# Head sums of both recurrence norms by exact block matrices in two passes, roots between 32x32 block transposes on VectorE

## The chip, the core and the metric

The kernel runs on one core of a Trainium2 chip. TensorE multiplies matrices (128 rows of contraction, results in PSUM banks of 512 fp32 columns), VectorE and ScalarE work on rows of 128 partitions, POOL and SyncE mostly issue transfers. Each engine takes its instructions in a fixed order, and waits between engines are semaphores. The metric is device time in microseconds (us); less is better. The time before is 1618.17 us, the median of three runs (1615.87 to 1621.76).

## The reference, cut to what matters

One layer of a hybrid decoder runs over 1024 prompt tokens and 8 groups of 8 sample tokens, 1088 columns in all. The change touches two norms of the recurrence branch, both over heads of 64 features:

```python
kk = heads(k * lp["k_k"])
kk = kk * lax.rsqrt(jnp.sum(kk * kk, axis=-1, keepdims=True) + 1e-12)
...
y, wkv_new = wkv7_scan(wkv_prev.astype(f32), rh, heads(decay), kh, vh, kk, ah)
mean = jnp.mean(y, axis=-1, keepdims=True)
var = jnp.mean(jnp.square(y - mean), axis=-1, keepdims=True)
y = ((y - mean) * lax.rsqrt(var + GN_EPS)).reshape(B, T, MIX_WIDTH)
y = y * lp["ln_w"].astype(f32) + lp["ln_b"].astype(f32)
bonus = jnp.sum(rh * kh * lp["r_k"].astype(f32), axis=-1, keepdims=True) * vh
y = (y + bonus.reshape(B, T, MIX_WIDTH)).astype(pr.dtype) * g
```

There are 8 heads, hence four blocks of 128 features (two heads each), f = 0 to 3. Around this stand one large input projection (1024 features to 4352), a pooling branch, a gated merge, an output projection and a squared-ReLU MLP.

## The kernel before, in words

Features lie on partitions and tokens along the free axis, so a row tile is 128 x 1088. The large products run in three single-pass products each: weights and activations are split into a high part (hi, rounded to the fp32r type) and a rest (lo), and hi x hi, hi x lo, lo x hi are summed in PSUM.

The first phase (`phase1`, up to about 755 us) has a *background* and *foreground* work on TensorE. The background is the input projection: 34 output blocks in two halves, 12 products for each three column chunks (364, 362, 362; `mm<-hx,whi` and `mm<-hx,wlo` in the trace), 2448 products, then 288 more for the merge's pooling part (`op_job`), 2736 in all. Its weights come as 128x512 loads on SyncE (L216) and are split by ScalarE (hi, L227) and VectorE or POOL (lo, L228); each split serves 36 products. The foreground is a set of generators: `chains`, `pools` (the pooling branch, one group of channels at a time: products, ScalarE copy L683, VectorE L684), `heads` (the recurrence) and `or_rows`. A planner, `Pace`, writes the program: it adds up a modelled time for every TensorE instruction and resumes a generator when its due time has come (`yield 2500` asks for 2.5 us of modelled time to pass); else it puts the next background product. So the order on TensorE is what the yields make it, and it is kept as written; the other engines' orders come from a scheduler. `pace.fill` puts one background triple between two foreground instructions.

`heads` goes through the four blocks. `front(f)` makes the normed key kk; `burst`, `scores`, `unit`, `bonus` prepare the products within chunks of 64 tokens; `inverse`, `level` and `affine` invert the chunks' triangular blocks; `chain` carries the state over the chunks (a state copy S on ScalarE, L1086, between TensorE products); `sample` does the sample tokens; `post(f)` is the group norm with scale, shift, bonus and gate. `post(f-1)` and `front(f+1)` run as a second generator beside `inverse`, `level` and `affine` of block f (`both`). `level` has a VectorE transpose (L961) whose result the next TensorE products (`hv,ao`) need.

The norms before. `rinv` is called nine times: in four fronts, three posts, and twice for the last post, which is done in two halves. Each call has for each 128 tokens a TensorE product with the *data block as weights* and two columns (`hsel`, one for each head) moving, in pairs between background triples. This gives the sums with tokens on partitions: 128 x 18 for the whole row. ScalarE takes the root (L396, with a table load), VectorE the reciprocal (L397), ScalarE expands each to 64 columns (L401) and loads the table of Tanh again by a dummy (L403); `spread` then transposes the expanded blocks back on TensorE (helper `tr`, L211), and VectorE multiplies from PSUM (L720 in the front, L1216 in the post). The mean of the post is an fp32 product with a 0/1 block matrix `bones` (helper `mm`, L204, `w<-wt,kct`), subtracted by VectorE (L1205) and squared by ScalarE (L1206); L1218 and L1219 add the shift and bonus and apply the gate; L1238 and L1239 split the result into hi and lo. The fp32r type is taken in one pass; these fp32 products are not.

At the end of the first phase the merge's operands come back by SyncE loads of 544 KB (`hx<-d_op`, L1416; `hx<-d_or`, L1428), and stored gate rows are reloaded on ScalarE's queue (`px<-d_th`, L1436).

The second phase (merge, output projection, MLP) keeps its TensorE instructions and their order.

## Time and profile before

| what | value |
|---|---|
| runs, median | 1618.17 us (1615.87 to 1621.76) |
| profiled execution | 1622.76 us, span 1621.0, mean granted TensorE clock 0.989 |
| TensorE busy | 1576.7 us, 97% |
| VectorE, ScalarE, POOL busy | 63%, 45%, 22% |
| stage 75 to 645 us (background and heads) | PE 561.18 of 570 |
| stage 645 to 755 us (last block, merge loads) | PE 104.16 of 110, clock 0.94 |

A row of a group reads: line, engine, operation, output<-inputs, shapes, count | busy us, mean ns of one | idle time ahead of it and what ended it. L204 and L211 are helpers that record every product and every transpose, so their groups are told apart by the tile names. An fp32 product has two records.

### The profile page before, as it was taken

The page shows a single profiled execution, that of the slowest core. Times are in us where ns is not written, and L with a number is a line of the kernel's source. Part 1 is how long each engine was busy: PE and PEld are TensorE (multiplying, and loading weights), DVE is VectorE, ACT ScalarE, POOL GpSimd, SP SyncE. Part 2 cuts the span into 40 slices and gives each one's busy share as a digit, 9 for nine tenths or more (in the row PEclk, how much of TensorE's full clock was granted, in tenths as well). Part 3 has the DMA queues.
Part 4 walks back from the last instruction along what each step waited for, and adds up shares of the span by engine and source line. Part 5 has one row for each costly group of instructions (what it writes and reads, how often), then busy time and mean ns, then how long its engine had stood idle before and what let it go on. Part 6 is the DMA issues. An engine that isn't in the chain of part 4 may idle for free.

```text
span 1621.0 us, 35482 instructions
## 1 busy us (share of the span) xinstructions
PE 1576.7 (97%) x14331; PEld 1472.5 (91%) x14331; DVE 1020.1 (63%) x1747; ACT 734.6 (45%) x1491; POOL 358.1 (22%) x464
## 2 busy tenths in 40 slices
PE   6999999999999999999999999999999999999997
PEld 3999878997898889879989999999999999999997
DVE  5685574756565636334635587776555677787866
ACT  5543343354334434432325475554445765553323
POOL 3301210020001000101513322333233343521221
PEclk9999999999999999899999999999999999999998
DMA  9334314333413242836874465667666965674313
GB/s 336 108 120 157 134 58 132 108 101 112 152 67 114 90 144 91 296 121 210 328 273 166 143 215 199 205 231 257 223 204 227 321 201 183 199 265 154 101 40 111
DMA packets 123380, 279.43 MB, mean 172 GB/s; under 512 B 16816, under 2 KB 31152, under 8 KB 123216
## 3 DMA queue, kind: packets, MB, share of 16 engines
q1 hardware_dynamic: 107856, 228.52, 41.2%
q0 software_dynamic: 9312, 32.41, 6.0%
q10 hardware_dynamic: 6048, 16.23, 2.9%
q8 instruction: 113, 1.85, 0.5%
q14 instruction: 51, 0.42, 0.1%
HBM read 198.15 MB, written 78.95 MB: 171 GB/s over the span
## 4 chain that ended last, share of the span: by engine, by line
PE 58%; DVE 3%; ACT 3%; issue 3%; DMA 2%; POOL 1%; POOLq 0%; ACTq 0%; SPq 0%; DVEq 0%
PE pr L204 30%; PE mm L204 20%; PE w L204 4%; PE wc L204 3%; DVE hx L1847 1%; DMA wraw<-in_w_out 1%; DMA d_hid<-hx 0%; DMA d_th<-px 0%; ACT whi L227 0%; POOL wlo L228 0%; PE w L211 0%; ACT hx L1770 0%; ACT mr L1770 0%; DVE wlo L228 0%; DMA d_orl<-wt 0%
## 5 line engine op out<-in xcount | busy, mean ns | idle before, releaser
L204 PE MATMUL mm<-hx,whi 128*128 128x362 f32 (+1 forms) x1920 | 509.6, 347 | 0.7 <-ACT px L573 0.7
L204 PEld LDWEIGHTS mm<-hx,whi 128*128 128x128 f32 x1920 | 333.5, 191 | 31.3 <-issue 13.0
L204 PE MATMUL pr<-mr,whi 128*128 128x272 f32 x1792 | 336.2, 287 | 0.2 <-DVE hx L1847 0.2
L204 PE MATMUL mm<-hx,wlo 128*128 128x362 f32 (+1 forms) x960 | 316.4, 330 | 0.0
L204 PEld LDWEIGHTS pr<-mr,whi 128*128 128x128 f32 x1792 | 280.6, 188 | 2.1 <-issue 2.1
L204 PE MATMUL pr<-mr,wlo 128*128 128x272 f32 x896 | 257.8, 288 | 0.0
L227 ACT ACTIVATE whi<-wraw 128x512 fp32r<-128x512 f32 x186 | 116.9, 629 | 204.6 <-PE mm L204 68.1
L228 DVE TENSOR_TENSOR wlo<-wraw,whi 128x512 fp32r<-128x512 f32 x145 | 108.4, 748 | 123.7 <-ACT whi L227 122.8
L204 PEld LDWEIGHTS mm<-hx,wlo 128*128 128x128 f32 x960 | 183.4, 191 | 0.0
L204 PE MATMUL pr<-hx,whi 128*128 128x272 f32 x896 | 168.8, 287 | 2.3 <-ACT hx L1650 0.9
L204 PEld LDWEIGHTS pr<-mr,wlo 128*128 128x128 f32 x896 | 168.6, 188 | 0.0
L204 PE MATMUL mm<-mr,whi 128*128 128x272 f32 (+4 forms) x736 | 152.3, 301 | 0.0
L204 PEld LDWEIGHTS pr<-hx,whi 128*128 128x128 f32 x896 | 140.2, 188 | 3.8 <-ACT hx L1650 1.1
L227 ACT ACTIVATE whi<-wr 128x512 fp32r<-128x512 f32 x138 | 86.3, 627 | 115.3 <-PE pr L204 76.7
L204 PE MATMUL pr<-hx,wlo 128*128 128x272 f32 x448 | 128.9, 288 | 0.0
L204 PEld LDWEIGHTS mm<-mr,whi 128*128 128x128 f32 x736 | 119.2, 188 | 3.0 <-issue 2.5
L204 PE MATMUL mm<-mr,wlo 128*128 128x272 f32 (+4 forms) x368 | 110.1, 299 | 0.0
L228 POOL TENSOR_TENSOR wlo<-wraw,whi 128x512 fp32r<-128x512 f32 x41 | 55.6, 1356 | 216.4 <-ACT whi L227 216.3
L228 DVE TENSOR_TENSOR wlo<-wr,whi 128x512 fp32r<-128x512 f32 x103 | 77.2, 752 | 19.2 <-ACT whi L227 19.2
L204 PE MATMUL pr<-t,whi 128*128 128x272 f32 x448 | 84.7, 287 | 0.7 <-DVE hx L1670 0.7
L204 PEld LDWEIGHTS pr<-hx,wlo 128*128 128x128 f32 x448 | 84.3, 188 | 0.0
L204 PEld LDWEIGHTS pr<-t,whi 128*128 128x128 f32 x448 | 70.1, 188 | 1.8 <-issue 1.8
(467 smaller groups left out, 2714.0 us busy)
## 6 DMA issues: line engine op xcount, KB each, us to landing
wr<-in_w_ff SPq DMA_DIRECT2D x137, 256.0 KB, 3.5
hid<-d_ch POOLq DMA_DIRECT2D x72, 272.0 KB, 3.8
wraw<-in_w_ff SPq DMA_DIRECT2D x71, 256.0 KB, 3.1
wraw<-in_w_in SPq DMA_DIRECT2D x68, 256.0 KB, 2.9
d_ch<-hx SPq DMA_DIRECT2D x52, 272.0 KB, 3.7
hid<-in_w_ada_mlp SPq DMA_DIRECT2D x24, 512.0 KB, 6.2
d_th<-px SPq DMA_DIRECT2D x22, 544.0 KB, 3.0
wt<-d_x SPq DMA_DIRECT2D x20, 544.0 KB, 3.8
```

Of the source, the lines that this page charges most:

```text
L204: return self.nc.tensor.matmul(out, lhsT, rhs, **kw)
L227: nc.scalar.activation(hi, raw, AF.Copy)
L228: (nc.gpsimd if pool else nc.vector).tensor_tensor(lo, raw, hi.bitcast(F32), op=ALU.subtract)
L1847: nc.vector.tensor_tensor(acc, acc, v, op=ALU.add)
```

## The change

Two helpers replace the old chain. `head_sums` makes the head sums as two fp32r products with a 0/1 block matrix that this type holds exactly: one with the data's hi part moving, one with its lo part, summed in PSUM. Every feature row of a head then holds the head's sum, with tokens along the free axis, so nothing has to be expanded. `apart` makes hi (ScalarE copy) and lo (VectorE subtraction). For the mean a second matrix `cen` (identity less 1/64 in each head's block) gives the centred value in the same two products; ScalarE squares it twice (once as fp32, once rounded) and copies it back, and VectorE makes the lo part of the square.

The roots: VectorE transposes the sums from PSUM in 32x32 blocks, so that one column of each block holds 32 different tokens; ScalarE takes the root of these columns (128 x 34 for the whole row), VectorE the reciprocal, and one VectorE transpose of the broadcast gives full rows again (128 x 1088, tile `e`). Then one multiplication of the whole row takes the place of the pieces.

The counts on TensorE: 72 products with two columns, 72 transposes and 12 fp32 mean products go; 72 fp32r products come, 24 of 512 and 48 of 288 columns. ScalarE's program has 15 instructions more, VectorE's 26. `bones` and `cen` are loaded on the POOL queue and rounded by ScalarE; the bonus sum keeps its fp32 product. hi and lo use the `wt` buffers. The bonus row's load moves behind `rinv` in the first three posts. The yields of the planner around all this change, and the order of pool and gate blocks in the background with them (two lines below stand for the yields). In the second phase nothing changes.

```diff
+KEEP = KC["bones"][0]
...
+    same = (r // 64) == (np.arange(P)[None] // 64)
+    put("bones", same)
+    put("cen", np.eye(P) - same / 64.0)
...
-    def rinv(self, x, blocks, scale, eps, R):
-
-        nc, k = self.nc, len(blocks)
-        ps = self.ps("w")
-        for i, b in enumerate(blocks):
-            if i and i % 2 == 0:
-                self.pace.fill()
-            self.mm(ps[:, 2 * i:2 * i + 2], x[:, b:b + 128], self.kc("hsel"), start=True, stop=True)
-        r = self.cp.tile([P, 10, 2], F32, tag="rh", bufs=3, name=self.nm("rh"))
-        last, r = r[:, 9, 0:1], r[:, :k, :]
-        f = r.rearrange("p k h -> p (k h)")
-        nc.scalar.activation(f, ps[:, :2 * k], AF.Sqrt, bias=self.eps[:, eps:eps + 1], scale=scale)
-        nc.vector.reciprocal(f, f)
-        i = 0
-        for x in R:
-            m = x.shape[1] // 128
-            nc.scalar.activation(x.rearrange("p (k h j) -> p k h j", h=2, j=64), r[:, i:i + m, :].unsqueeze(3).to_broadcast([P, m, 2, 64]), AF.Copy)
-            i += m
-        nc.scalar.activation(last, R[-1][:, 0:1], AF.Tanh)
-        return [x[:, o:o + 128] for x in R for o in range(0, x.shape[1], 128)]
-
-    def spread(self, R):
-
-        ps = self.ps("w")
-        for i, x in enumerate(R):
-            self.tr(ps[:, i * 128:(i + 1) * 128], x, self.kc("ident"))
-        return ps
+    def head_sums(self, w, hi, lo, s):
+
+        ps, n = self.ps("w"), s.stop - s.start
+        self.mm(ps[:, :n], w, hi[:, s], start=True, stop=False)
+        self.mm(ps[:, :n], w, lo[:, s], start=False, stop=True)
+        return ps[:, :n]
+
+    def rinv(self, x, hi, lo, cuts, scale, eps):
+
+        nc, a, b = self.nc, cuts[0].start // 32, cuts[-1].stop // 32
+        for s in cuts:
+            nc.vector.transpose(x[:, s], self.head_sums(self.bones, hi, lo, s))
+            yield 500
+        r = self.cp.tile([P, 2, 34], F32, tag="rh", bufs=2, name=self.nm("rh"))
+        q, r = r[:, 0, :b - a], r[:, 1, :b - a]
+        nc.scalar.activation(q, cut32(x)[:, a:b, 0], AF.Sqrt, bias=self.eps[:, eps:eps + 1], scale=scale)
+        nc.vector.reciprocal(r, q)
+        nc.scalar.activation(q[:, 0:1], q[:, 0:1], AF.Tanh)
+        nc.vector.transpose(cut32(x)[:, a:b, :], r.unsqueeze(2).to_broadcast([P, b - a, 32]))
+
+    def apart(self, x, hi, lo, s):
+
+        nc = self.nc
+        nc.scalar.activation(hi[:, s], x[:, s], AF.Copy)
+        nc.vector.tensor_tensor(lo[:, s], x[:, s], hi[:, s].bitcast(F32), op=ALU.subtract)
+
+    def wtr(self):
+        return self.row(self.p1, "wt", 5, F32R)
+
+    def spare(self):
+        return self.row(self.p1, "e", 1, w=1112)[:, :NT]
 
...
-            yield (8500, 9800, 9800, 10800)[g]
+            yield (9500, 11000, 11500, 10800)[g]
...
-        kk = self.wt()
+        sq, hi, lo = self.spare(), self.wtr(), self.wtr()
         for c0, n in FH:
-            nc.scalar.activation(kk[:, c0:c0 + n], k[:, c0:c0 + n], AF.Square, scale=self.par("k_k", f))
+            nc.scalar.activation(sq[:, c0:c0 + n], k[:, c0:c0 + n], AF.Square, scale=self.par("k_k", f))
+            self.apart(sq, hi, lo, slice(c0, c0 + n))
         yield X(12)
         wa = self.wt()
         nc.sync.dma_start(wa, self.d_x[12])
-        t1, tha = self.wt(), self.wt()
-        yield self.pace.warm(FW if f else 11000)
-
-        R = self.rinv(kk, self.blocks(0, NT), 1.0, 1, [kk[:, 0:512], kk[:, 512:1024], t1[:, 0:128]])
-        yield 2500
-        for i, (c0, n) in enumerate(((0, 512), (512, 512), (1024, 64))):
-            ps = self.spread(R[4 * i:4 * i + 4])
-            o = 64 if i == 2 else 0
-            nc.vector.scalar_tensor_tensor(kk[:, c0:c0 + n], k[:, c0:c0 + n], self.par("k_k", f), ps[:, o:o + n], op0=ALU.mult, op1=ALU.mult)
-            yield 800
+        yield FW if f else 14500
+
+        yield from self.rinv(sq, hi, lo, FS, 1.0, 1)
+        kk, t1, tha = self.wt(), self.wt(), self.wt()
+        nc.vector.scalar_tensor_tensor(kk, k, self.par("k_k", f), sq, op0=ALU.mult, op1=ALU.mult)
+        yield 1000
...
-            self.mm(ps[:, :n], self.kc("bones"), q[:, c0:c0 + n], start=True, stop=True)
+            self.mm(ps[:, :n], self.bones.bitcast(F32), q[:, c0:c0 + n], start=True, stop=True)
...
-        yield self.pace.warm(3000)
+        yield self.pace.warm(3500)
...
-        sq = self.wt()
-        bv = self.wt()
-        nc.sync.dma_start(bv, self.d_bv[f])
-        if not last:
+        hi, lo, sq = self.wtr(), self.wtr(), self.spare()
+
+        def bonus():
+            bv = self.wt()
+            nc.sync.dma_start(bv, self.d_bv[f])
+            return bv
+
+        if last:
+            bv = bonus()
+        else:
             if f < 2:
                 self.got = self.fetch(f + 2)
-            yield 5000
+            self.apart(y, hi, lo, slice(0, NT))
+            yield 5200
...
-            for a, m in FP:
-                if c0 <= a < c0 + n:
-                    s = slice(a, a + m)
-                    ps = self.ps("w")
-                    self.mm(ps[:, :m], self.kc("bones"), y[:, s], start=True, stop=True)
-                    nc.vector.scalar_tensor_tensor(y[:, s], ps[:, :m], -1.0 / 64, y[:, s], op0=ALU.mult, op1=ALU.add)
-                    nc.scalar.activation(sq[:, s], y[:, s], AF.Square)
-                    yield 1500
-            yield self.pace.warm(2500 if last else 3500)
-            end = c0 + n == NT
-            R = self.rinv(sq, self.blocks(c0, n), 1.0 / 64, 2, [sq[:, a:a + 512] for a in (0, 512) if c0 <= a < c0 + n] + [g2] * end)
-            yield 3000 if last else 4000
-            for i, a in enumerate(a for a in (0, 512) if c0 <= a < c0 + n):
-                for b, m, o, blk in ((a, 512, 0, R[4 * i:4 * i + 4]), (NPR, 64, 64, R[-1:]))[:1 + (a > 0)]:
-                    ps = self.spread(blk)
-                    t = y[:, b:b + m]
-                    nc.vector.scalar_tensor_tensor(t, t, self.par("ln_w", f), ps[:, o:o + m], op0=ALU.mult, op1=ALU.mult)
-                s = slice(a, NT if a else 512)
-                nc.vector.scalar_tensor_tensor(y[:, s], y[:, s], self.par("ln_b", f), bv[:, s], op0=ALU.add, op1=ALU.add)
-                nc.vector.tensor_tensor(y[:, s], y[:, s], sg[:, s], op=ALU.mult)
-                yield 1000
+            cuts = [x for x in FS if c0 <= x.start < c0 + n]
+            if last:
+                for x in cuts:
+                    self.apart(y, hi, lo, x)
+                yield 2000
+            for x in cuts:
+                ps = self.head_sums(self.cen, hi, lo, x)
+                nc.scalar.activation(sq[:, x], ps, AF.Square)
+                nc.scalar.activation(hi[:, x], ps, AF.Square)
+                nc.scalar.activation(y[:, x], ps, AF.Copy)
+                nc.vector.tensor_tensor(lo[:, x], sq[:, x], hi[:, x].bitcast(F32), op=ALU.subtract)
+                yield 800
+            yield 2500 if last else 3500
+            yield from self.rinv(sq, hi, lo, cuts, 1.0 / 64, 2)
+            s, b = slice(c0, c0 + n), bv if last else bonus()
+            nc.vector.scalar_tensor_tensor(y[:, s], y[:, s], self.par("ln_w", f), sq[:, s], op0=ALU.mult, op1=ALU.mult)
+            nc.vector.scalar_tensor_tensor(y[:, s], y[:, s], self.par("ln_b", f), b[:, s], op0=ALU.add, op1=ALU.add)
+            nc.vector.tensor_tensor(y[:, s], y[:, s], sg[:, s], op=ALU.mult)
...
          else:
+            yield 1500
             yield from norm(0, NT)
-            hi, lo = sq.bitcast(F32R), y.bitcast(F32R)
+            lo = y.bitcast(F32R)
             nc.scalar.activation(hi, y, AF.Copy)
             nc.vector.tensor_tensor(lo, y, hi.bitcast(F32), op=ALU.subtract)
             nc.sync.dma_start(self.d_or[0][f], hi.bitcast(F32))
...
-        for g in range(4):
-            jobs += [Q[g], G[2 * g], G[2 * g + 1]] if g < 3 else [G[6], Q[3], G[7]]
-        jobs += G[8:]
+        gates = iter(G)
+        jobs += [Q[int(x)] if x in "0123" else next(gates) for x in "0gg1gggg2ggg3"]
+        jobs += list(gates)
...
+        two = sm.tile([P, 2 * P], F32R, name="bones")
+        raw = self.hv()[:, :2 * P]
+        nc.gpsimd.dma_start(raw, io["kc"][:, KEEP:])
+        nc.scalar.activation(two, raw, AF.Copy)
+        self.bones, self.cen = two[:, 0:P], two[:, P:]
...
-FW = 5500
+FW = 8500
```

On TensorE, at the second block's norm. `wc_5970` collects the sums of squares, `mm` is background:

```order
L204 MATMUL mm_5795<-hx_352,wlo_5687 128x362
L204 MATMUL wc_5970<-kct,wt_5588 128x2 x2
L204 MATMUL mm_5793<-hx_354,whi_5759 128x364
L204 MATMUL mm_5793<-hx_355,whi_5759 128x364
L204 MATMUL mm_5793<-hx_354,wlo_5760 128x364
```

and some 30 instructions later a pool group's last products (`px`, `ds` with `plw`), the transposes of the roots and the products of a later block's inverse (`z,hv`):

```order
L204 MATMUL w_6058<-px_5615,plw_5222 128x298
L204 MATMUL w_6058<-ds_5786,plw_5222 128x64
L211 MATMUL wc_6063<-kct,wt_5588 128x128 x4
L204 MATMUL wc_6071<-z,hv_6042 32x32 x32
L211 MATMUL w_6108<-kct,wt_5588 128x128 x4
L211 MATMUL w_6114<-kct,sw_5582 128x128
L204 MATMUL mm_5794<-hx_358,whi_5759 128x362
```

Now the sums of the same norm (`wt_5527` is hi, `wt_5528` lo) between products of the inverse:

```order
L206 MATMUL wc_5730<-hv_5669,hv_5509 32x32 x64
L206 MATMUL wc_5797<-wt_5527,bones 128x512
L206 MATMUL wc_5797<-wt_5528,bones 128x512
L206 MATMUL mm_5617<-hx_358,whi_5607 128x362
L206 MATMUL mm_5617<-hx_359,whi_5607 128x362
L206 MATMUL mm_5617<-hx_358,wlo_5608 128x362
L206 MATMUL mm_5618<-hx_358,whi_5607 128x362
L206 MATMUL mm_5618<-hx_359,whi_5607 128x362
L206 MATMUL mm_5618<-hx_358,wlo_5608 128x362
L206 MATMUL w_5807<-wt_5527,bones 128x288
L206 MATMUL w_5807<-wt_5528,bones 128x288
```

The pool group's products no longer stand here, and nothing on TensorE comes back for the roots.

On VectorE, beside block 3's `level`. Before, with the mean subtractions (`wc_7536` to `w_7594`) and the transpose (L961):

```order
L1205 SCALAR_TENSOR_TENSOR wt_7432<-wc_7536,wt_7432 128x512
L1205 SCALAR_TENSOR_TENSOR wt_7432<-wc_7564,wt_7432 128x288
L228 TENSOR_TENSOR wlo_7574<-wraw_7571,whi_7573 128x512
L1205 SCALAR_TENSOR_TENSOR wt_7432<-w_7594,wt_7432 128x288
L954 TENSOR_TENSOR hv_7672<-w_7607,kct 128x512
L228 TENSOR_TENSOR wlo_7766<-wraw_7763,whi_7765 128x512
L961 STREAM_TRANSPOSE hv_7757<-wc_7692 128x512
L397 RECIPROCAL rh_7803<-rh_7803 128x18
L1216 SCALAR_TENSOR_TENSOR wt_7432<-wt_7432,part,wc_7938 128x512
```

Now, with the three transposes of the sums, the reciprocal, the transpose of the roots and L965, the former L961:

```order
L230 TENSOR_TENSOR wlo_7467<-wraw_7464,whi_7466 128x512
L958 TENSOR_TENSOR hv_7555<-wc_7490,kct 128x512
L398 STREAM_TRANSPOSE e_7293<-w_7557 128x512
L398 STREAM_TRANSPOSE e_7293<-w_7567 128x288
L398 STREAM_TRANSPOSE e_7293<-wc_7577 128x288
L403 RECIPROCAL rh_7652<-rh_7652 128x34
L405 STREAM_TRANSPOSE e_7293<-rh_7652 128x1088
L965 STREAM_TRANSPOSE hv_7646<-wc_7581 128x512
L1226 SCALAR_TENSOR_TENSOR wt_7284<-wt_7284,part,e_7293 128x1088
```

The transpose for the inverse stood ahead of the reciprocal and now stands behind the whole chain of the roots.

At the end of the first phase, on ScalarE, with the state copies S and the reload of a gate row. Before:

```order
L227 ACTIVATE whi_8096<-wraw_8094 128x512
L1086 ACTIVATE S_8155<-wc_8121 128x64
L1436 DMA px_8396<-d_th_101 128x1088
L1086 ACTIVATE S_8182<-wc_8121 128x64
L1086 ACTIVATE S_8197<-wc_8121 128x64
```

Now:

```order
L1090 ACTIVATE S_8167<-wc_7949 128x64
L1099 ACTIVATE wt_7272<-wc_7950 128x512
L410 ACTIVATE wt_8046<-wt_7272 128x512
L1450 DMA px_8268<-d_th_99 128x1088
L1090 ACTIVATE S_8237<-wc_8203 128x64
```

On SyncE, the merge's loads and the last gate row's write there (`d_th_105`), before:

```order
L1428 DMA hx_7884<-d_orh_74 128x1088
L1428 DMA hx_7886<-d_orl_78 128x1088
L1428 DMA hx_7888<-d_orh_75 128x1088
L1428 DMA hx_7890<-d_orl_79 128x1088
L608 DMA d_th_105<-px_7581 128x1088
L216 DMA wraw_8264<-in_w_br 128x512
L1186 DMA wt_8228<-d_bv_69 128x1088
```

Now:

```order
L1442 DMA hx_8144<-d_orh_74 128x1088
L1442 DMA hx_8146<-d_orl_78 128x1088
L1442 DMA hx_8148<-d_orh_75 128x1088
L1442 DMA hx_8150<-d_orl_79 128x1088
L1442 DMA hx_8152<-d_orh_76 128x1088
L1442 DMA hx_8154<-d_orl_80 128x1088
L614 DMA d_th_105<-px_7801 128x1088
L218 DMA wraw_8373<-in_w_br 128x512
```

All six loads of recurrence rows now stand ahead of that write; before, two came later.

More of the change, by code (lines that the diff above doesn't have):

```diff
@@ L541, in rest @@
                 round_(qi, 1)
-                yield from vectors(qi, 2600 if qi == 1 else 1800)
+                yield from vectors(qi, 2100 if qi == 1 else 1300)
                 rows(qi)
@@ L1060, in affine @@
         self.done.add(("s", f, 1))
-        yield 3600
+        yield 3300
     def chain(self, f, d):
@@ L1158, in sample @@
             ums.append(um)
-        yield 4500
+        yield 5000
         pn = self.ps("w")
@@ L1330, in run @@
             nc.gpsimd.dma_start(self.part, io["par"])
-            self.kct = self.cp.tile([P, NKC], F32, name="kct")
-            nc.gpsimd.dma_start(self.kct, io["kc"])
+            self.kct = self.cp.tile([P, KEEP], F32, name="kct")
+            nc.gpsimd.dma_start(self.kct, io["kc"][:, :KEEP])
             self.eps = self.cp.tile([P, 3], F32, name="eps")
```

12 lines of the change are left out of this document (6 added, 6 removed).

## Prediction

> **What bounds the kernel now.** I read the page first (busy shares, the forty slices, the chain that ended last), then a table by stage, then the chain and the timelines around each norm, then the costliest groups of VectorE and ScalarE by shape.
>
> ```profile
> span 1621.0 us, 35482 instructions
> PE 1576.7 (97%) x14331; PEld 1472.5 (91%) x14331; DVE 1020.1 (63%) x1747; ACT 734.6 (45%) x1491; POOL 358.1 (22%) x464
> PE   6999999999999999999999999999999999999997
> PE 58%; DVE 3%; ACT 3%; issue 3%; DMA 2%; POOL 1%; POOLq 0%; ACTq 0%; SPq 0%; DVEq 0%
> ```
>
> TensorE is busy 97% of the span and the chain that ended last runs mostly over it, so a microsecond less on TensorE is a microsecond less in the end, unless a wait takes its place. VectorE has a third of its time free, ScalarE half. By stage (the columns are length, busy time and instructions of PE, PEld, DVE, ACT and POOL, granted clock, DMA share, GB/s):
>
> ```profile
> 75.00:645.00 570.00, 561.18 (x6185) 496.94 (x6184) 351.45 (x651) 242.46 (x582) 47.72 (x99) 0.99 0.34 112
> 645.00:755.00 110.00, 104.16 (x1276) 92.94 (x1275) 40.09 (x74) 38.60 (x78) 9.78 (x9) 0.94 0.56 198
> 755.00:910.00 155.00, 154.41 (x1152) 147.87 (x1151) 82.45 (x134) 56.08 (x93) 53.65 (x52) 1.00 0.70 250
> ```
>
> The change acts in the first two rows, where background products and the head pipeline share TensorE. There 570.0 - 561.2 + 110.0 - 104.2 = 14.6 us are idle. The rest is work, so that is where most of a gain must come from. Everything after 755 us keeps its instructions; I cost it at nothing.
>
> **Removed from TensorE.** First the sums of squares, the block of data as weights and two columns moving, in pairs between three background products (start, duration, two records for each product); then one mean product of 288 columns; then transposes of the expanded roots in the last norm.
>
> ```profile
> 494.59 0.50 PE L204 MATMUL wc<-kct,wt 128*128 128x2 f32 x4
> ...
> 495.53 0.50 PE L204 MATMUL wc<-kct,wt 128*128 128x2 f32 x4
> 481.97 0.65 PE L204 MATMUL wc<-wt,kct 128*128 128x288 f32 x2
> ...
> 482.95 0.49 PE L204 MATMUL mm<-hx,whi 128*128 128x362 f32 x2
> 746.36 0.44 PE wc L211 x4
> 746.80 0.11 PE w L211
> 746.91 7.94 PE mm L204 x48
> 944.97 179.84 PE pr L204 x1443
> ```
>
> A background product of 362 columns takes 7.94 / 48 = 0.165 us, three 0.50. A pair and three background products take 495.53 - 494.59 = 0.94, so one sum product is (0.94 - 0.50) / 2 = 0.22; there are 72: 15.8 us. The mean product and three background products take 482.95 - 481.97 = 0.98, so 288 columns cost 0.48, and 512 by the same rate 0.48 x 512 / 288 = 0.85; 8 and 4 of them: 7.3 us. Five transposes take 746.91 - 746.36 = 0.55, or 0.11 each; 72: 7.9 us. Together 31.0 us.
>
> **Added to TensorE.** 72 single-pass products (hi and lo for each of three pieces, over nine root chains and the four centrings), 24 of 512 and 48 of 288 columns. No product of before in this form has these widths; the nearest are the background's own: 0.165 for 362 columns, and 179.84 / 1443 = 0.1246 for 272, both 0.00046 a column. So 288 columns cost 0.132 and 512 0.234: 6.3 + 5.6 = 11.9 us. From below 10% less (no fixed part); from above the price of the fp32 means, 48 x 0.48 + 24 x 0.85 = 43.4. I take the low end, since products of this type are the row it is nearest to. Net: -19.1 us.
>
> **The stall in the second block's norm.** Before, the root chain and a pool group met (chain pieces, PE timeline, and three windows with PE busy, granted clock, DMA share, GB/s):
>
> ```profile
> 500.22 1.28 ACT L396
> 502.13 1.15 ACT wt L401 x2
> 505.16 1.28 ACT L403
> 504.61 0.77 PE L204 MATMUL w<-px,plw 128*128 128x298 f32 x2 [1.85 <-DVE px L684]
> 507.93 1.12 PE L211 MATMUL w<-kct,wt 128*128 128x128 f32 x4 [0.47 <-DVE px L684]
> 503.00:513.00 10.00, 7.78 (x89) 0.68 0.46 153
> 658.50:670.00 11.50, 10.54 (x98) 0.57 0.78 296
> 691.00:697.50 6.50, 4.80 (x29) 0.75 0.33 110
> ```
>
> TensorE waited 1.85 + 0.47 us for a pool copy that stood behind two table loads (L396, L403) and the expansions (L401), and then ran 10 us at 0.68 of its clock, 3.2 us lost. After the change the pool group's products have other due times, the expansions are gone, and no TensorE instruction needs the transposed roots at once. I take the whole -5.5 us, with 0 as the other end (the stall turns up at another place).
>
> [...]
>
> **Added wait in the block inverse.** In the three norms beside a later block's inverse, VectorE's order now has the reciprocal and the 1088-column transpose of the roots ahead of the transpose (L961 before, L965 after) that TensorE's next coupling products need; before, that one came first. The chain from the third head sum to it, in before's rows:
>
> ```profile
> L396 ACT ACT_TABLE_LOAD x9 | 11.5, 1283 | 0.2
> L396 ACT ACTIVATE rh<-wc,eps 128x18 f32<-128x18 f32 x4 | 1.1, 278 | 6.8 <-PE wc L204 6.8
> L397 DVE RECIPROCAL rh<-rh 128x18 f32<-128x18 f32 x7 | 1.9, 265 | 18.4 <-ACT rh L396 18.4
> L474 DVE STREAM_TRANSPOSE sq<-sq 128x512 f32<-128x512 f32 x2 | 1.4, 682 | 3.2 <-ACT sq L472 3.2
> L961 DVE STREAM_TRANSPOSE hv<-wc 128x512 f32<-128x512 f32 x2 | 1.4, 716 | 5.8 <-PE wc L204 5.8
> 490.94 1.63 PE L204 MATMUL w<-iv,hv 32*32 32x32 f32 x128
> 492.50 0.60 PE L204 MATMUL mm<-hx,whi 128*128 128x362 f32 x2
> ```
>
> Transpose of 288 columns 0.682 x 288 / 512 = 0.38, table load 1.28, root 0.28, reciprocal 0.3, transpose of 1088 columns 0.682 x 1088 / 512 = 1.45, the awaited transpose 0.72: 4.4, some 0.2 of hand-overs, and about 1.3 if an instruction is already running on ScalarE and on VectorE: 5.9. TensorE's cover is the products between (492.50 - 490.94 = 1.56) and 21 background products, 3.5: 5.1. So 0.8 us of wait, 1.3 with some clock lost: three times, +4 us. From below 0 (the chain wins by 0.5); from above, with a wait of 2.7 and 1.6 of slow clock as in the tail below, 4.3 x 3 = +13.
>
> **VectorE, ScalarE, the queues.**
>
> ```profile
> L1239 DVE TENSOR_TENSOR wt<-wt,wt 128x1088 fp32r<-128x1088 f32 x3 | 3.9, 1286 | 3.4 <-ACT wt L1238 3.4
> L1205 DVE SCALAR_TENSOR_TENSOR wt<-w,wt 128x512 f32<-128x512 f32 x2 | 1.4, 692 | 0.3 <-PE w L204 0.3
> L1205 DVE SCALAR_TENSOR_TENSOR wt<-w,wt 128x288 f32<-128x288 f32 x5 | 2.3, 457 | 3.9 <-PE w L204 3.9
> L401 ACT ACTIVATE wt<-rh 128x512 f32<-128x512 f32 x16 | 9.3, 622 | 4.5 <-DVE rh L397 4.4
> L1238 ACT ACTIVATE wt<-wt 128x1088 fp32r<-128x1088 f32 x3 | 3.3, 1098 | 0.0
> ```
>
> VectorE gets two transposes of 1088 columns for each of eight full chains (16 x 1.45 = 23) and twelve subtractions of hi (12 x 1.29 = 15), and loses the mean subtractions (4 x 0.69 + 8 x 0.46 = 6); its multiplications are regrouped. So about +32 us in the first two stages, from (351.5 + 40.1) / 680 = 58% busy to 62%. ScalarE gets some 16 passes of 1088 (16 x 1.1 = 18) and loses the 9.3 us of expansions: +9, 41% to 43%. Both are hidden by their idle time, except at the places named. The cover to watch is the split of w_in's weights, lo on VectorE: each serves 36 products (6 us) and there are two buffers, so a chain of 4 us ahead of a split does not empty TensorE. The load of the bonus moves behind the root chain in three norms, on SyncE's queue past a few weight loads; the multiplication that needs it is the second on VectorE after the roots, and a weight split stands behind that. The 544 KB would have to come more than those 6 us late to reach TensorE; nothing. The two block matrices come by one load on the POOL queue and a ScalarE copy at the start, long before use: nothing.
>
> **The tail of the first phase.** The last block's chain and the loads of the merge stage's operands (8 `hx<-d_op`, then 4, now 6, `hx<-d_or`) collide in both versions.
>
> ```profile
> 651.82 1.85 issue
> 658.90 0.96 issue
> 692.43 0.22 ACT L1086 ACTIVATE S<-wc 128x64 f32<-128x64 f32 x1 [6.70 <-DMA d_th<-px]
> 692.70 0.33 PE L204 MATMUL wc<-S,ra 64*64 64x64 f32 x4 [2.73 <-ACT S L1086]
> hx<-d_oph SPq DMA_DIRECT2D x4, 544.0 KB, 7.3
> ```
>
> Each load took some 7 us to land, and before, the collision cost 1.85 + 0.96 of "issue", 11.5 x 0.43 = 4.9 of clock around 660, then a state copy stuck behind a gate reload on ScalarE's queue (2.73 and 6.5 x 0.25 = 1.6 of clock): 12.0 us. After, the head pipeline ends earlier against the background (product 2601 of 2736, before 2694), 14 loads stand together ahead of the last gate write on SyncE, and a gate's reload, into the buffer that this last write has to release, stands on ScalarE just ahead of the first state copy of the second unit. So the same kind of block falls on the chain of block 3. I take it as unchanged, from -12 (nothing meets) to +12 (twice as much).
>
> **Sum.** -19.1 - 5.5 + 4 + 0 = -20.6 us. The profiled execution took 1622.76 us, 1.7 more than its span and 4.6 above the median 1618.17: 1602.2 for it, 1597.6 on the median.
>
> **Rivals.**
> - *The tail goes too.* The pipeline's earlier end leaves more background behind it to fill its waits. -20.6 - 12 = -32.6: 1585. For it: the pipeline ends 93 background products earlier. Against it: two more loads in the same burst. 0.17.
> - *The slow clock stays* with another cause: -19.1 - 2.3 + 4 = -17.4: 1601. For it: the idleness before it was short; against it: in all three windows above slow clock follows on a PE wait. 0.10.
> - *A wait in place of the work.* The block inverse at its upper end (+13) or the tail at +12: -9 to -12, 1606 to 1610. For it: the order on VectorE; against it: VectorE 62% busy. 0.16. Both together: -20.6 + 9 + 12 = about 0: 1618, no change; 0.07.
> - *Slower.* TensorE takes hi and lo only when ScalarE and VectorE have made them, and there is one more hand-over in each norm. If every one of the nine chains holds TensorE as the state copy did (2.73 + 1.6 = 4.3), that is 39 us against 24.6: +14, 1632. It decides from 24.6 / 9 = 2.7 us a chain. Against it: the planned time from a split to its first product is 2 us or more in all nine, filled with background. 0.05, with which I count the case that the products run at the fp32 price (+31.5: -20.6 + 31.5 = +11, 1629), which the background's 0.165 us all but excludes.
>
> **How the numbers follow.** The forecast's own case has the remaining 0.45, range 1590 to 1604. Faster: 0.45 + 0.17 + 0.10 + 0.16 = 0.88; within 0.3% (4.9 us, about what a measurement of this kernel can tell from no change) 0.07; slower 0.05. The range leaves out the slower case, no change, and the outer part of the tail's gain, some 0.17: 1582 to 1611.
>
> **What would show it.** Right: no matmul with 2 columns and no L211 group on the norms' tiles; head-sum products near 0.13 and 0.23 us; clock near 1.0 at the second block's norm; PE busy in the stage down by about 19; waits on the inverse's transpose (L965) of a microsecond, three times. Wrong: these waits at 3 us and more, followed by half clock; PE waits on hi or lo at the norms; an idle or half-clock stretch of over 15 us while the merge operands load; a weight split late behind a root chain.

## The result, and the profile after

The changed kernel takes 1596.98 us in the median of four runs (1593.93 to 1598.03); the kernel before, with one more run, 1617.17. The ratio is 0.9867, 95% interval 0.9842 to 0.9892: 20.2 us less, where 20.6 were forecast. The profiled execution took 1598.03 us, span 1596.3. Its page (busy shares, granted clock by slice, shares of the chain that ended last):

```profile
span 1596.3 us, 35169 instructions
PE 1555.4 (97%) x14163; PEld 1451.1 (91%) x14163; DVE 1055.0 (66%) x1773; ACT 743.8 (47%) x1506; POOL 364.5 (23%) x465
PEclk9999999999999999999999999999999999999999
PE 57%; DVE 3%; issue 2%; ACT 2%; DMA 1%; POOL 1%; DVEq 0%; SPq 0%; POOLq 0%; ACTq 0%
```

VectorE is busier by 35 us and ScalarE by 9, as worked out (+32, +9), TensorE less by 21, still at 97%. To split the gain I cut both traces at the first product of the output projection (`mm<-mr`), which stands at the same place of the work; from here on "first phase" means all that stands ahead of it, the merge included. The table by stage up to it (length, busy time and instructions by engine, granted clock, DMA share, GB/s), before and then after:

```profile
0.00:801.30 801.30, 771.35 (x8069) 681.27 (x8070) 468.25 (x848) 329.47 (x738) 109.97 (x193) 0.98 0.44 148
```

```profile
0.00:771.90 771.90, 746.88 (x7901) 657.15 (x7902) 502.00 (x874) 337.85 (x752) 115.88 (x194) 0.99 0.45 154
```

The first phase is 29.4 us shorter. TensorE's idle time went from 801.3 - 771.4 = 30.0 to 771.9 - 746.9 = 25.0 us. Up to the cut the granted clock of both traces is 1.00 or 0.50. The stretches at 0.50 last 3.41, 6.83 or 10.24 us, so I count them in steps of 3.41 us: eight before (one from 18.41, one from 230.04, two from 506.52, three from 660.12, one from 694.25 us), three after (two from 342.94, one from 540.92). So 13.3 us lost to the clock became 5.1 (half of the busy time inside them). What is left is work at full clock: 801.3 - 30.0 - 13.3 = 758.0 and 771.9 - 25.0 - 5.1 = 741.8. So 16.2 us are work, 5.0 idle time, 8.2 clock; of the clock, 1.7 are a step at 18 us, ahead of everything that the change touches. The second phase was 5.5 us *longer* to the last product in this execution, with unchanged instructions: the same split gives equal work (805.1 and 805.2), 2.3 us more of idle time and 3.1 of clock. The two profiled executions differ by 24.7 us of span where the medians differ by 20.2, so the split tells of these two executions, and its terms are not those of the median.

The new products, between background triples (start, duration, one record each):

```profile
81.50 0.62 PE L206 MATMUL w<-wt,bones 128*128 128x512 f32 x2
...
82.94 0.42 PE L206 MATMUL w<-wt,bones 128*128 128x288 f32 x2
...
84.20 0.43 PE L206 MATMUL wc<-wt,bones 128*128 128x288 f32 x2
```

Six background products (0.99 us) stand between them: (82.94 - 81.50 - 0.99) / 2 = 0.225 us for 512 columns, (84.20 - 82.94 - 0.99) / 2 = 0.135 for 288. The forecast had 0.234 and 0.132.

Stretches in which the clock was low before or is low now (length, PE busy, granted clock, DMA share, GB/s); the first row is of before, the others of after:

```profile
645.00:715.00 70.00, 64.16 (x994) 0.90 0.62 223
```

```profile
503.00:513.00 10.00, 10.00 (x136) 1.00 0.26 84
645.00:715.00 70.00, 70.00 (x659) 1.00 0.69 248
342.50:350.00 7.50, 7.50 (x85) 0.54 0.80 253
540.50:544.50 4.00, 3.99 (x19) 0.57 0.00 0
882.00:889.50 7.50, 6.75 (x33) 0.54 0.28 87
```

The stall at 503 us is gone, and the whole tail too: 70 of 70 us busy at full clock. New slow stretches stand at 342 and 540, each after one of these waits, which before were under 1 us or not there (engine, tile and line that waited <- what it waited for: total, times, longest):

```profile
PE mm L206 <- ACT px L579: 2.6, 1, 2.6
PE w L206 <- DVE px L660: 2.5, 1, 2.5
PE mm L206 <- ACT px L630: 1.9, 1, 1.9
```

The first stands at 76 us with no slow clock behind it, the second at 538, the last at 340. The last is the new split's doing. ScalarE's timeline ahead of it:

```profile
335.37 2.39 ACT L970 ACTIVATE z<-wc 32x512 f32<-32x512 f32 x4 [0.86 <-DVE hv L965]
337.78 1.39 ACT L715 ACTIVATE e<-wt,part 128x512 f32<-128x512 f32 x2
339.20 1.19 ACT L981 ACTIVATE hv<-wc 32x512 f32<-32x512 f32 x2
340.42 1.20 ACT L410 ACTIVATE wt<-e 128x512 fp32r<-128x512 f32 x2
341.65 0.47 ACT L630 ACTIVATE px<-mm 128x364 f32<-128x364 f32 x1
342.17 0.60 PE L206 MATMUL mm<-hx,whi 128*128 128x362 f32 x2 [1.95 <-ACT px L630]
```

The inverse's copies, a front's squares and the hi copies of the split (L410) hold ScalarE for 6.2 us, and the copy of a finished background block (L630), which frees TensorE's bank, stands behind them. In `one_fp32_product`, below, which leaves the hi copies out and keeps the rest of this queue, TensorE waits 0.41 us at this place in place of 1.95.

### The profile page after: what moved, and what is told of

Read it like the earlier page. It is cut to its first block, busy times and chain, and to the rows that moved or that the text cites. A ratio compares the mean times of both kernels' runs of the same rounds, so it can differ in the third digit from the quotient of the medians.

```text
span 1596.3 us, 35169 instructions
## 1 busy us (share of the span) xinstructions
PE 1555.4 (97%) x14163; PEld 1451.1 (91%) x14163; DVE 1055.0 (66%) x1773; ACT 743.8 (47%) x1506; POOL 364.5 (23%) x465
## 4 chain that ended last, share of the span: by engine, by line
PE 57%; DVE 3%; issue 2%; ACT 2%; DMA 1%; POOL 1%; DVEq 0%; SPq 0%; POOLq 0%; ACTq 0%
PE pr L206 30%; PE mm L206 20%; PE w L206 4%; PE wc L206 3%; DVE hx L1861 1%; DMA wraw<-in_w_out 0%; DMA hid<-d_u 0%; ACT whi L229 0%; ACT hx L1784 0%; DMA wr<-in_w_ff 0%; DVE hx L2030 0%; DVE wlo L230 0%; ACT mr L1784 0%; DVE hx L1785 0%; POOL wr L1834 0%
## 5 line engine op out<-in xcount | busy, mean ns | idle before, releaser
L206 PE MATMUL mm<-hx,whi 128*128 128x362 f32 (+1 forms) x1920 | 499.7, 342 | 5.2 <-ACT px L579 2.6
L206 PEld LDWEIGHTS mm<-hx,whi 128*128 128x128 f32 x1920 | 332.2, 189 | 42.4 <-issue 20.2
```

What stands on the lines that cost most here:

```text
L206: return self.nc.tensor.matmul(out, lhsT, rhs, **kw)
```

## The experiments

Theory after the result: the work taken off TensorE is worth its own time, and the rest of the gain is idle time and slow clock, which fall where due times put them. Rivals are named with each run. The column "work, idle, clock" is the split above, up to the output projection, from each run's profiled execution. Work repeats within about 2.6 us between kernels with the same TensorE instructions (741.8 to 744.4); part of this is the input norm's products ahead of 75 us (`mm<-sq,ones`), which the change does not touch and which take 7.6 to 11.2 us in these runs.

| run | median us | ratio to before, interval | first phase: length = work + idle + clock |
|---|---|---|---|
| before | 1617.17 | | 801.3 = 758.0 + 30.0 + 13.3 |
| changed | 1596.98 | 0.9867 [0.9842, 0.9892] | 771.9 = 741.8 + 25.0 + 5.1 |
| products_twice | 1603.00 | 0.9915 [0.9893, 0.9937] | 781.7 = 753.6 + 24.7 + 3.4 |
| one_fp32_product | 1605.09 | 0.9925 [0.9905, 0.9945] | 781.9 = 753.3 + 24.4 + 4.2 |
| late_block3 | 1594.77 | 0.9859 [0.9838, 0.9880] | 772.0 = 744.0 + 24.6 + 3.4 |
| old_plan | 1612.74 | 0.9971 [0.9959, 0.9982] | 789.1 = 744.4 + 35.5 + 9.2 |
| front_due_old | 1612.16 | 0.9964 [0.9948, 0.9979] | 788.5 = 744.3 + 33.4 + 10.8 |
| pools_old | 1601.73 | 0.9900 [0.9881, 0.9919] | 778.4 = 743.7 + 27.6 + 7.0 |
| fronts_only | 1619.01 | 1.0018 [1.0004, 1.0032] | 800.2 = 756.6 + 40.1 + 3.5 |
| posts_only | 1614.12 | 0.9976 [0.9962, 0.9989] | 789.8 = 753.4 + 33.0 + 3.4 |
| jobs_only | 1627.34 | 1.0064 [1.0048, 1.0080] | 810.5 = 758.4 + 37.8 + 14.2 |
| roots_twice | 1599.46 | 0.9885 [0.9869, 0.9901] | 773.1 = 743.1 + 28.3 + 1.7 |
| late_post2 | 1603.70 | 0.9919 [0.9906, 0.9933] | 781.6 = 744.1 + 29.9 + 7.6 |
| pool2_later | 1594.14 | 0.9861 [0.9848, 0.9874] | 772.5 = 744.2 + 24.9 + 3.4 |

**What a product costs: products_twice, one_fp32_product.**

```diff
         self.mm(ps[:, :n], w, lo[:, s], start=False, stop=True)
+        self.nc.tensor.matmul(ps[:, :n], w, hi[:, s], start=True, stop=False)
+        self.nc.tensor.matmul(ps[:, :n], w, lo[:, s], start=False, stop=True)
```

> The changed kernel with every head-sum pair issued twice (72 more fp32r products, 24 of 512 and 48 of 288 columns, into the same bank with the same result); the planner is not told, so all orders stay. Theory (TensorE's work in the first phase is the time): 24 x 0.226 + 48 x 0.132 = 11.8 us more than the changed kernel, 1607 to 1611. Rival (the norms are held by the splits and the root chains, and products lie in their shade): under 5 us more.

The first phase grew by 9.8 us, its work by 11.8 as worked out, its idle time and clock shrank by 2.0. The norms' products themselves hold 11.9 us more. The median rose by only 6.0, below the range I gave (7.8 by the ratios, whose intervals allow 2 to 13). So the cost of a product is shown, and in this execution's first phase it counts nearly in full; that it does so in the median is not shown.

In the next one `hi` is the unsplit data:

```diff
-        self.mm(ps[:, :n], w, hi[:, s], start=True, stop=False)
-        self.mm(ps[:, :n], w, lo[:, s], start=False, stop=True)
+        self.mode = (P, P)
+        for _ in range(2):
+            self.pace.spend(n / 2.4 + 14, 1)
+        self.nc.tensor.matmul(ps[:, :n], w.bitcast(F32), hi[:, s], start=True, stop=True)
...
-            self.apart(sq, hi, lo, slice(c0, c0 + n))
```

> The changed kernel with each head sum as one fp32 product of the unsplit data in place of two fp32r products; the splits for the sums and the second square are left out, the planner counts the same time, so the order stays nearly the same. Theory (TensorE work): 36 sums cost 12 x 0.85 + 24 x 0.48 = 21.7 us against 11.8, so +10 us, 1604 to 1610. Rival (VectorE and ScalarE work, 15 and 18 us of it gone here, holds TensorE in the first phase): no slower than the changed kernel, 1590 to 1598.

8.1 us slower in the median, 10.0 in the first phase, with 11.5 more work, 10.2 of it on these products. VectorE did 17 us less in the first phase and ScalarE 13, and TensorE's idle time fell by no more than 0.6: the wait at 340 us shrank, the one near 540 grew from 2.5 to 3.3. So the two passes with their splits are worth 8 to 10 us against one fp32 product, and VectorE's added work is hidden, as forecast.

**The plan: old_plan, front_due_old, pools_old, jobs_only.** `old_plan` takes all yields and the job order of before with the new norms; `front_due_old` only this:

```diff
-        yield FW if f else 14500
+        yield FW if f else 11000
...
-FW = 8500
+FW = 5500
```

> The new norms with the due times of the kernel before and its order of pool and gate blocks. Theory (the work taken from TensorE is the gain, the plan only decides where idle time falls): 19 us of work less, and stalls of another size, 1595 to 1605. Rival (the retuned plan brings the larger part): 1608 or more.

> The changed kernel with only the fronts' due times as before (first product of the key norm 5.5 in place of 8.5 us of planned time after the split is issued, 11 in place of 14.5 in block 0). Theory (with the old plan TensorE waited 2 to 2.3 us three times for hi on ScalarE, L410, and ran at half clock after it; the due time is what removed that): 6 to 10 us slower than the changed kernel, 1602 to 1608, waits on L410. Rival (the pool groups' place made the old plan slow): within 3 us of the changed kernel.

The rival of the first won: with the old plan the new norms gain 4 us in place of 20, and the fronts' due times alone bring it to the same 1612. The work is as low as in the other runs with these norms, but idle time and clock rise by 14 to 15 us. For the second the direction was right and my range, up to 1608, too small. The waits in `front_due_old`, and one of them on ScalarE and TensorE:

```profile
PE w L206 <- ACT wt L410: 5.2, 3, 2.6
PE w L206 <- DVE ra L1035: 4.9, 3, 2.3
PE w L206 <- DVE wt L411: 1.8, 2, 1.0
338.96 1.20 ACT L410 ACTIVATE wt<-e 128x512 fp32r<-128x512 f32 x2
339.64 0.50 PE L206 MATMUL w<-wt,bones 128*128 128x512 f32 x1 [2.60 <-ACT wt L410]
```

The same queue of ScalarE as at 342 us above, only that here TensorE comes for hi itself 3 us earlier. A later due time does not shorten the queue; it puts background ahead of the product. Waits on hi and lo (L410, L411) are 7.0 us of this run's idle time. The 4.9 us on L1035 are not, and why they come with these due times stays open.

`pools_old` undoes the pool groups' yields and the order of pool and gate blocks; `jobs_only` puts that order alone into the kernel before:

```diff
-            yield (9500, 11000, 11500, 10800)[g]
+            yield (8500, 9800, 9800, 10800)[g]
...
-        gates = iter(G)
-        jobs += [Q[int(x)] if x in "0123" else next(gates) for x in "0gg1gggg2ggg3"]
-        jobs += list(gates)
+        for g in range(4):
+            jobs += [Q[g], G[2 * g], G[2 * g + 1]] if g < 3 else [G[6], Q[3], G[7]]
+        jobs += G[8:]
```

> The changed kernel with only the pool groups' due times and the background's order of pool and gate blocks as before. Theory (of the plan, the fronts' due times carry nearly all, 15 us; the pool groups' place is worth what they stalled in the kernel before, up to 5): 1594 to 1602. Rival (root chains and pool groups meet again, as at 503 us before): 1605 to 1612, with a wait of some 2 us on a pool copy and half clock after it.

> The kernel before with only the new order of pool and gate blocks in the background. Theory (the norms' work is what is gone, and before's stalls stay with its norms): within 4 us of the kernel before, 1613 to 1621. Rival (the meeting of a pool group with the roots at 503 us goes by this order alone): 1609 to 1613, without the wait of 1.85 us and the slow clock near 505 us.

The pool groups' place is worth some 5 us, the upper end of the theory's range (the two intervals overlap a little), and as the rival said there is a wait on the pool group's VectorE result (L690, 2.5 us, up to 502) with slow clock around it (0.71 from 486 to 506 us). Alone on the old norms the new order costs 10, which neither side expected: the stall at 503 goes, and two of 4.6 and 5.1 us come, at 467 and 554, each on a pool group (TensorE's waits, then one instruction):

```profile
PE w L204 <- issue: 6.9, 2, 5.1
467.31 1.55 PE L204 MATMUL w<-px,plw 128*128 128x364 f32 x2 [4.55 <-DVE hv L923]
```

In both runs a part of the plan, taken without the chains that it was made for, loses.

**One norm at a time: fronts_only, posts_only.** The other norm is put back as it was before, with its own products and transposes; in `posts_only` with the fronts' old due times.

> Only the key norms of the four fronts in the new form, with the new plan; the group norms as before (fp32 mean products, two-column sums, transposes back). Theory (the work taken from TensorE counts for each norm alike): 36 x 0.22 + 36 x 0.11 - 8 x 0.226 - 16 x 0.132 = 8.0 us of work less than the kernel before, and stalls that may fall either way by 5: 1604 to 1613. Rival (the group norms are what stalled TensorE before, or the plan is what counts): no gain, 1614 or more.

> Only the group norms in the new form, with the new plan but the fronts' own norms and due times as before. Theory: 36 x 0.22 + 36 x 0.11 + 7.3 - 16 x 0.226 - 32 x 0.132 = 11.4 us of work less, and the tail's stalls (some 10 us of idle time and half clock between 650 and 700 us) gone, since the last norm is the new one: 1594 to 1606. Rival (the tail's stalls went by chance of the order): 1605 or more.

No gain for the one and 3 us for the other, both outside the theory's range. Work fell in both (by 1.4 and 4.6, against 8.0 and 11.4 worked out; in the first, 3.3 us of the difference are the input norm's products in the first 75 us, which the change does not touch; what else keeps the work up in both is not known), and idle time rose by 10 and 3; `fronts_only` has a single stop of 11.6 us on a pool group. These runs hold a plan that was made for the whole, so they don't tell the share of each norm. They do tell that the parts' gains don't add up to the whole.

**The tail: late_block3, late_post2.**

```diff
+            if f == 3:
+                yield 12000
```

> The changed kernel with 12 us of planned time put ahead of block 3, so that the last head sum stands at background product 2685 of 2736 in place of 2601 (2673 in the kernel before). Theory (the stalls of the tail went because block 3's chain no longer runs while the merge's operands load and the gates are reloaded): 6 to 12 us of idle time and half clock come back between 645 and 715 us: 1603 to 1609. Rival (they went because the last norm's chain is shorter or does not use ScalarE in the same way): within 3 us of the changed kernel.

The theory fell. Block 3's chain now runs as late as before, and the tail stays full:

```profile
645.00:715.00 70.00, 69.27 (x795) 1.00 0.60 217
```

Next I followed what had held the state copy before: the chain at 680 us runs from the write of block 2's result on SyncE over the gate row's write to its reload on ScalarE. SyncE's timeline, before and after:

```profile
679.27 0.32 SPq L1240 DMA_DIRECT2D d_orh<-wt  x1
...
684.96 0.38 SPq L1439 DMA_DIRECT2D d_th<-px  x1
```

```profile
636.23 0.32 SPq L1249 DMA_DIRECT2D d_orh<-wt  x1
...
676.45 0.32 SPq L1453 DMA_DIRECT2D d_th<-px  x1
```

Block 2's norm ends 43 us earlier and its writes no longer stand between the loads and the gate rows. `late_post2` brings this order back:

```diff
-            yield 1500
+            yield 24000 if f == 2 else 1500
             yield from norm(0, NT)
```

> The changed kernel with 24 in place of 1.5 us of planned time ahead of block 2's group norm, so that the writes of its result stand on SyncE behind the merge's first loads and ahead of a gate row's write, as in the kernel before. Theory (before, that late result held SyncE's queue, the gate row's write and its reload on ScalarE, and the state copy behind the reload; this is the 2.7 us of idle time and the slow clock near 692 us): an idle stretch of 2 us or more ahead of a state product (S, ra) between 650 and 700 us and 3 to 8 us on the time, 1600 to 1605. Rival (the tail's stalls had another cause): no such wait, 1594 to 1599.

It costs 6.7 us, as foreseen, but by another wait: block 3's norm waits 5.13 us for the load of its gate input, and the granted clock around it is 0.62. TensorE's row, the window, then a wait of SyncE's queue and the rows that end it:

```profile
667.83 1.55 PE L206 MATMUL w<-wt,sw 128*128 128x364 f32 x2 [5.13 <-DMA wt<-d_x]
664.00:673.00 9.00, 5.17 (x18) 0.62 0.74 238
SPq L1184 <- PE w L206: 5.0, 1, 5.0
661.18 0.53 PE L206 MATMUL w<-wt,bones 128*128 128x288 f32 x2
661.75 0.32 SPq L1184 DMA_DIRECT2D wt<-d_x  x1
...
674.85 0.32 SPq L1249 DMA_DIRECT2D d_orh<-wt  x1
```

The load (L1184) goes into a `wt` buffer, of which there are five, and SyncE waited 5.0 us for it, up to block 2's last head sum, which read hi and lo from `wt`. The write of block 2's result (L1249) comes only after the stall. So a late group norm of block 2 costs what I named, but here by the buffers that it holds and not by the write of its result; the theory's mechanism was not tested. That it is what stopped the state copy before is read from the chain of before and not reproduced. In the runs with the old group norm (`fronts_only`, `jobs_only`) the wait on the state copy is there again between 640 and 720 us, 1.5 and 3.1 us; in the eleven with the new one it is 0.2 us once and absent otherwise. So it goes with the old group norm; which part of that norm brings it stays open.

**VectorE's chain: roots_twice.**

```diff
-        nc.vector.transpose(cut32(x)[:, a:b, :], r.unsqueeze(2).to_broadcast([P, b - a, 32]))
+        for _ in range(2):
+            nc.vector.transpose(cut32(x)[:, a:b, :], r.unsqueeze(2).to_broadcast([P, b - a, 32]))
```

> The changed kernel with VectorE's transpose of the broadcast roots done twice in each of the nine chains, 1.31 us each time, ahead of the inverse's transpose (L965) in the three posts. Theory (the chain ends well before TensorE comes for L965, so the wait that I priced at 4 us is not there): within 2 us of the changed kernel, no wait on L965. Rival (the chain is at its limit): 3 x 1.3 us and half clock after it, +4 to +13.

2.5 us slower, inside the noise of the two, and no wait on L965. The scheduler put L965 between the two transposes, not behind both, so the run shows that 8 x 1.3 us more of VectorE's work are hidden but for 1.2 us of the first phase, and not how close the chain is to its limit. That is read from the changed kernel, in the next section.

**A remaining stall: pool2_later.**

```diff
-            yield (9500, 11000, 11500, 10800)[g]
+            yield (9500, 11000, 12500, 10800)[g]
```

> The changed kernel with the third pool group due 1 us later (12.5 us of planned time in place of 11.5), against the 2.5 us that TensorE waits near 540 us for the group's edge columns on VectorE. Theory (each stall left is a matter of one due time): the wait shrinks by about 1 us and with luck the slow clock after it goes, 1593 to 1597. Rival: the same work is late elsewhere, no change.

The wait near 540 us shrank from 2.47 to 1.47 us, by the 1 us foreseen, and the first background product behind it takes 0.61 us where the changed kernel, at half clock there, takes 1.05. That the shorter wait is the reason is not shown: in the changed kernel 2.56 us of waiting near 76 us had no slow clock behind them either. Changed kernel, then this one:

```profile
540.51 1.15 PE L206 MATMUL w<-px,plw 128*128 128x364 f32 x2 [2.47 <-DVE px L660]
540.92 1.05 PE L206 MATMUL mm<-hx,whi 128*128 128x364 f32 x1
```

```profile
541.38 0.85 PE L206 MATMUL w<-px,plw 128*128 128x364 f32 x2 [1.47 <-DVE px L660]
541.79 0.61 PE L206 MATMUL mm<-hx,whi 128*128 128x364 f32 x1
```

1594.14 is the lowest median here, against 1596.98; the intervals overlap, so it isn't shown to be faster.

## Why the prediction was right, point by point

The time came out within a microsecond, but not by its terms. The work gained less than forecast, new stalls came, the wait in the inverse did not come, the tail's stalls went, and the second phase was longer; these misses cancelled. That TensorE's work is the largest term was right; that the sum fits within a microsecond is luck.

- **Work on TensorE** (-19.1): -16.2 by the split of the changed kernel, about -14 against the other runs' work; without the input norm's products it is -14 to -16 in all of them. An added product is as priced (0.225 and 0.135 us; 11.9 us more when doubled). The removed two-column products were mis-sized: their share of the trace before, by starts and ends at full clock, is 12.3 us, or 0.17 each, where pairs between triples gave 0.22; the transposes have 9.1 for 7.9, the means 7.3 as worked out. By the same share the 72 added products hold 14.1 us and not 11.9, so by shares the term is 14.1 - 28.7 = -14.6. Mis-sized are thus the two-column products and, by shares, the added ones; why an added product holds more time in its place than a second one right behind it stays open.
- **The stall at 503** (-5.5): gone, 10 of 10 us busy at full clock. But waits of the same size came at 76, 340 and 538 us (7.0 us, and 5.1 of clock). At the first two a hi copy (L410) stands ahead of the copy that TensorE waits for; the third is a pool group's, and moves with its due time (`pool2_later`). I had only asked what the removed stall would become, not what the new hi copies would delay on ScalarE.
- **The wait in the inverse** (+4): it isn't there. The rows of one such place:

```profile
331.11 0.42 PE L206 MATMUL w<-wt,bones 128*128 128x288 f32 x2
331.97 0.48 DVE L398 STREAM_TRANSPOSE e<-w 128x288 f32<-128x288 f32 x1
331.34 1.28 ACT L402 ACT_TABLE_LOAD   x1
332.64 0.35 ACT L402 ACTIVATE rh<-e,eps 128x34 f32<-128x34 f32 x1
333.02 0.37 DVE L403 RECIPROCAL rh<-rh 128x34 f32<-128x34 f32 x1 [0.58 <-ACT rh L402]
333.42 1.31 DVE L405 STREAM_TRANSPOSE e<-rh 128x1088 f32<-128x1088 f32 x1
334.66 0.68 DVE L965 STREAM_TRANSPOSE hv<-wc 128x512 f32<-128x512 f32 x1
336.34 1.20 PE L206 MATMUL wc<-hv,ao 32*32 32x32 f32 x64
```

From the last head sum (ends 331.53) to the end of L965 (335.34) are 3.8 us where I had 5.9; TensorE comes at 336.34, 1.0 later. At the other two places the chain takes 4.3 and 3.3 us, and TensorE comes 0.6 and 2.2 us after its end. The step that failed is the sum of the chain: the table load ran wholly or partly beside or ahead of the transposes (here most of its 1.28 us is off the chain, at the tightest place only 0.2), and the 1.3 us for busy engines was not needed. The cover, here 4.8 us, was about as worked out (5.1).
- **The tail** (0, -12 to +12): its lower end came, some 13 us: 5.8 of idle time and, by four steps of 3.41 us at half clock, 6.8 of clock. That was the rival "the tail goes too", with the wrong reason: `late_block3` shows that the earlier end of the pipeline is not the cause.
- **The rest of the kernel** (0): +5.5 in the profiled execution, all of it idle time and clock. In the fourteen profiled executions the second phase takes 809.4 to 817.7 us with its work at 804.4 to 805.8, so zero was right for the work. The three with the old group norm take 809.4 to 812.2, the eleven with the new one 810.1 to 817.7; whether the change lengthens this phase by a wait stays open. Where 3.1 us of the +5.5 fell is in the last section.
- **The slower rival's mechanism** is real. TensorE does wait for hi, three times for 2.0 to 2.3 us in `old_plan` and for up to 2.6 in `front_due_old`, and runs slowly around it (granted clock 0.79 from 338 to 346 us in `front_due_old`). The fronts' old due times cost 15 us of the 20; in that run's trace the waits on hi and lo are 7.0 us, and the rest is other idle time and slow clock. I dismissed it because every planned time was 2 us or more. The fact that mattered is how long ScalarE's queue is at that place: 5.5 us of plan were too short, 8.5 enough.
- **The slow clock** as a rival of its own: the stretch at 503 did go with its stall. All slow stretches of the first phase, before and after, follow on waits, the shortest of 0.75 us (229 us, before). One reading was wrong: the step at 506.52 us began ahead of the second piece of idleness, 0.47 us up to 507.93, so 1.85 us stood before the slow clock and not 1.85 + 0.47.

## What to carry to other kernels

Price a replaced operation by TensorE's work, but then walk each new input of a product back through the queues of the engines that make it, and ask what stands ahead of it there and what stands behind it: here the same new products were worth 5 us or 20, by the due times of the fronts. Where an order is written out by due times, an edit and its plan are one change; test them together, and don't read the share of a part from a run with the whole's plan. A total that fits is no proof of its terms: cut both traces at the same instruction and compare work, idle time and clock apart.

## What the runs showed of the hardware

In the changed kernel's trace a wait of 2.47 us at 538 us and one of 1.95 at 340 have half clock behind them, and in the trace of before one of 0.75 at 229. A longer one has none: ahead of block 0's norm, near 76 us, TensorE of the changed kernel waits 2.56 us, and the clock stays at 1.00 up to 342.94. So in these traces the length of a wait alone does not tell whether slow clock follows; what does is not shown. At the start of the MLP the same two waits stand in both kernels; rows of the changed kernel, and of `late_block3`:

```profile
879.83 1.28 PE L206 MATMUL wc<-kct,t 128*128 128x5 f32 x10 [1.24 <-DVE t L1541]
884.41 0.79 PE L206 MATMUL pr<-hx,whi 128*128 128x272 f32 x2 [0.75 <-DVE rs L2056]
```

```profile
879.86 1.28 PE L206 MATMUL wc<-kct,t 128*128 128x5 f32 x10 [1.13 <-DVE t L1544]
883.89 0.49 PE L206 MATMUL pr<-hx,whi 128*128 128x272 f32 x2 [0.78 <-DVE rs L2059]
```

In the first, a slow stretch of 6.8 us begins at 882.25, behind the first wait and ahead of the second (the row 882 to 889.5 above); in the second execution there is none: a pair of hi products takes 0.41 us at 885.11, where the changed kernel's takes 0.65 at 885.23. That is 3.0 us (half of the 6.1 busy ones inside) between two executions whose first waits differ by a tenth of a microsecond. In `pool2_later` and in the kernel before the first wait is 0.74 and 0.59 us, and no slow stretch follows in either.
